# The order of the mixer's input projections: four output gate tiles placed between tiles with convolutions, and the triangular systems appended one tile sooner

## The chip, the cores and the metric

The kernel runs on one core of one Trainium2 chip. The metric is device time in microseconds. The kernel before took 2859.01 us, the median of 3 runs (2853.66 to 2862.34).

## What is computed

One layer of a decoder for 1024 prompt tokens and 8 sequences of 4 sample tokens, 1056 token columns in all, width 1024:

```
x += 1/2 * gate1 * SwiGLU1(mod(RMSNorm(x)))
h  = mod(RMSNorm(x))
qkv, z, b, a, q_raw, ckv_raw, kr_raw = split(h @ w_in)     # the input projection
qkv = silu(causal_conv(qkv)); q, k = l2_norm(q), l2_norm(k)
M   = strict_lower(beta * k k^T * decay);  T = inv(I + M)  # the triangular systems
o   = gated_delta_rule(q, k, v, T, ...) normed, times silu(z)
mla = attention over latents (q_raw, ckv_raw, kr_raw) and the paged cache
x += gate2 * [o, mla] @ w_out
x += 1/2 * gate3 * SwiGLU2(mod(RMSNorm(x)))
```

The change lies in the mixer's input projection `h @ w_in` and in what hangs on it.

## The kernel before

The features of `h` lie on the partitions, the 1056 token columns in four blocks of 264. The stage `mixer_in` (L1241) works through `w_in` in tiles of 128 columns. `ORDER` (L44) names them: `k0`..`k3`, `q0`..`q3` and `v0`..`v3` are the tiles of keys, queries and values that go through a convolution; `m0`..`m5` are the queries of the latent attention, `c0` its latents, and `z0`..`z3` the output gates. `I0` and `F0` are no tiles: they append side work to a list.

`proj` (L659) makes one tile: 4 blocks of 24 matmuls (each product in three parts, L127 to L129, out `pp`), and after each block an evacuation on ACT: L876 (`raw`) for k, q and v, L691 for m and c, L1228 (`zt<-pp`, a SiLU) for z. A z tile has no further work than one DMA, issued from ACT's queue (L1229). The weights of the tile two ahead are loaded on SP's queue (L648, `wraw`), cast on ACT (L652, `whi`), and their low parts are made on POOL (L101, `wlo`).

After each block `proj` calls `hook` (L682), which takes every generator on the list `active` one step further. So the side work is written between the blocks of later tiles:

- A tile of k, q or v appends its chain: `taps` (L881: ACT L893, three DVE passes L895, ACT L897 and L898), then nine transposes on PE (`ptk<-raw`, L701). For k and q follow the token norm (ACT L911, DVE L912, small DVE operations L707 to L720, DVE L920 `tok`), a scaling on POOL (`cy<-tok,egc`), transposes back on PE (`pch<-tok`, `pch<-cy`, L935), their evacuation (ACT L936) and products on PE (`pk`, L947).
- `I0` appends `invert` (L1040), which starts when all four k chains are done: masking on POOL (`M<-M,bi`), 31 steps of two DVE operations (`inv<-M` L1064, `M<-M,inv` L1066), and stores (POOL `X<-M,low`).
- `F0` appends nine times `mla_q_finish` (L1130), called F tiles below, three steps each, which start when the six m tiles are done: a load (SP, `mq<-qr_d`, L1138), squares (ACT L1140), sums and a root on DVE (L1143 to L1148), a scaling on POOL (`mq<-mq,g_q`), rotations on DVE and POOL (L1088 to L1093, `rp`), and a store (`qc_d<-mq`, L1153).

A framework lays the instructions out on every engine's queue by a schedule that it works out at build time; each queue then runs in that order. POOL is the exception: in this stage it keeps the order in which the code is written. The next stage, the attention of `mixer_heads`, begins when the last tile is done; its first transposes are `pqk` and `pqa`.

In a few words, of `mixer_in` and of `hook`:

```python
elif t[0] == "z":
    self.proj_z(m, tp, ps)
elif t[0] == "I":
    self.active.append(self.once("k", 4, self.invert(ml, tp)))
elif t[0] == "F":
    self.active.append(self.once("m", 6, self.in_turn([self.mla_q_finish(t, tp, ml) for t in range(NTL)])))
...
for g in list(self.active):
    if next(g, done) is done:
        self.active.remove(g)
```

Of the kernel before, what the change touches and what calls it, by code (L numbers as in the profile page):

```python
# [40 lines left out]
            ("T1", "S1", "Y", False), ("T4", "A22", "Z", True), ("B22", "S4", "Y", True))  # L41


ORDER = "k0 k1 m0 m1 k2 k3 c0 m2 I0 m3 m4 m5 F0 q0 q1 q2 q3 v0 v1 v2 v3 z0 z1 z2 z3"  # L44

PSQ = 3
WENG = 1
# [37 lines left out]
class Kernel:  # L85
# [1145 lines left out]
    def mixer_start(self):  # L1231
# [4 lines left out]
        first = {"k": 512, "q": 0, "v": 1024, "c": 2832, "m": 2064, "z": 1536}  # L1236
        self.worder = [[(2048, 16), (2960, 32)]] + [[(first[t[0]] + int(t[1]) * P, P)] for t in ORDER.split() if t[0] in first]
        while len(self.wready) < WFIRST:
            self.wready.append(self.proj_weights(WENG and self.nc.vector))

    def mixer_in(self):  # L1241

        nc, tc = self.nc, self.tc
        order = ORDER.split()
        c = self.keep
# [318 lines left out]
    def mla_prompt_gen(self, tp, ps):  # L1564
# [79 lines left out]
        def pv(h, qc, k, off, hi, lo):  # L1644

            vhi, vlo = va[h % 2]
            if k == 0:
                pas[h, qc] = ps.tile([P, 512], F32, tag="V", name="pa")
            last = k == ORDER[qc][-1]
            self.mm3(pas[h, qc][:, off:], vhi[:, k], vlo[:, k], hi[:, off:], lo[:, off:], k == 0, last)  # L1650
# [29 lines left out]

        ORDER = ((0, 3, 2, 1), (0, 7, 6, 5, 1, 2, 3, 4))

        def products(h):

            T = qk[h % 2]
            for qc in range(2):
                for k in ORDER[qc]:
                    off = max(0, k - 4 * qc) * P
# [569 lines left out]
```

## Time and profile before

| what | us |
|---|---|
| median of 3 runs | 2859.01 |
| the profiled execution, its own time | 2863.72 |
| its span, first to last instruction | 2861.9 |
| PE busy in the span | 2673.6 (93%) |
| DVE busy | 1766.6 (62%) |
| POOL busy | 1083.2 (38%) |
| ACT busy | 1074.2 (38%) |
| m2's first block to the end of z3 | 969 to 1286 |

PE runs the matmuls, PEld loads their weights, DVE, ACT and POOL do the elementwise work, SP issues DMAs. Times of rows are microseconds from the span's start. In brackets at a row's end stands how long the engine had been idle before it, and what it waited for. PEclk is the clock granted to PE, as a share of the full one.

### The profile page before, as it was taken

Reading aid. Unit: us, or ns where it says so; the run is one execution under the profiler, and the core shown is the slowest. Engines: PE = TensorE matmul, PEld = TensorE weight load, DVE = VectorE, ACT = ScalarE, POOL = GpSimd, SP = SyncE. Lnnn points to the kernel's source line nnn. Section 1 sums busy time; section 2 is a strip of 40 time slices with the busy share of each in tenths; the row PEclk is TensorE's granted clock in tenths of the full one; section 3 lists DMA queues with packets and bytes.
Section 4 is the critical chain, followed back from the end, with each engine's and each line's share of the span. In section 5 each row is a group of like instructions: output and inputs, shape, how many; then the busy total and the mean of one; then the engine's idle time right before and its main releaser. Section 6 shows DMA issues by size and latency. Waiting matters only on the chain.

```text
span 2861.9 us, 53475 instructions
## 1 busy us (share of the span) xinstructions
PE 2673.6 (93%) x21536; PEld 2462.5 (86%) x21536; DVE 1766.6 (62%) x3490; ACT 1074.2 (38%) x2005; POOL 1083.2 (38%) x1032
## 2 busy tenths in 40 slices
PE   4999999989999897799999988998979999999999
PEld 3888989989999787787877866776979999999999
DVE  7644445465574688847767677777585555546555
ACT  5322223211144443324656664543443333322111
POOL 0222222233352555544434466452433333323331
PEclk7999999999999998898999998987979999999999
DMA  7554353243232473432212144222522222224322
GB/s 272 154 163 134 120 162 105 81 161 106 76 109 77 149 206 117 141 110 78 63 42 58 49 96 114 83 64 53 188 82 82 76 87 71 90 82 167 98 76 69
DMA packets 339490, 308.35 MB, mean 108 GB/s; under 512 B 93865, under 2 KB 282017, under 8 KB 336171
## 3 DMA queue, kind: packets, MB, share of 16 engines
q1 hardware_dynamic: 304837, 246.32, 28.4%
q10 hardware_dynamic: 28262, 37.64, 4.1%
q0 software_dynamic: 6144, 20.98, 2.3%
q8 instruction: 169, 2.77, 0.4%
q14 instruction: 78, 0.64, 0.1%
HBM read 229.29 MB, written 75.59 MB: 107 GB/s over the span
## 4 chain that ended last, share of the span: by engine, by line
PE 42%; DVE 8%; issue 5%; POOL 4%; DMA 2%; ACT 1%; SPq 0%; ACTq 0%; POOLq 0%; DVEq 0%
PE po L128 4%; PE po L129 4%; PE po L127 4%; PE pY L127 2%; PE pY L128 2%; PE pY L129 2%; PE kraw L127 2%; PE pX L127 2%; PE pX L128 2%; PE pX L129 1%; PE pZ L127 1%; PE pZ L129 1%; PE pZ L128 1%; PE kraw L129 1%; PE kraw L128 1%
## 5 line engine op out<-in xcount | busy, mean ns | idle before, releaser
L127 PE MATMUL po<-act,whi 128*128 128x264 f32 x1408 | 402.4, 286 | 6.4 <-DVE x L435 4.7
L129 PE MATMUL po<-act,wlo 128*128 128x264 f32 x1408 | 403.2, 286 | 0.0
L128 PE MATMUL po<-act,whi 128*128 128x264 f32 x1408 | 402.0, 286 | 0.0
L435 DVE SCALAR_TENSOR_TENSOR x<-po,modT,x 128x264 f32<-128x264 f32 (+1 forms) x416 | 195.2, 480 | 238.8 <-PE po L129 238.3
L127 PEld LDWEIGHTS po<-act,whi 128*128 128x128 f32 x1408 | 266.8, 189 | 7.1 <-DVE x L435 4.9
L129 PEld LDWEIGHTS po<-act,wlo 128*128 128x128 f32 x1408 | 266.1, 189 | 0.0
L128 PEld LDWEIGHTS po<-act,whi 128*128 128x128 f32 x1408 | 265.9, 189 | 0.0
L370 POOL TENSOR_TENSOR A<-wg,A 128x512 fp32r<-128x512 f32 x84 | 111.0, 1321 | 372.1 <-ACT A L369 372.1
L127 PE MATMUL pp<-hhi,whi 128*128 128x264 f32 (+1 forms) x768 | 223.9, 292 | 4.5 <-DVE nt L354 3.6
L128 PE MATMUL pp<-hlo,whi 128*128 128x264 f32 (+1 forms) x768 | 223.7, 291 | 0.0
L129 PE MATMUL pp<-hhi,wlo 128*128 128x264 f32 (+1 forms) x768 | 221.8, 289 | 0.0
L2001 DVE TENSOR_REDUCE kss<-ksq 128x8 f32<-128x512 f32 x256 | 173.1, 681 | 69.7 <-ACT ksq L2000 67.7
L127 PE MATMUL pX<-B,A 128*128 128x264 f32 x704 | 203.9, 290 | 10.6 <-ACT B L369 9.7
L111 POOL TENSOR_TENSOR wlo<-wraw,whi 128x1024 fp32r<-128x1024 f32 x39 | 97.7, 2510 | 305.2 <-ACT whi L108 305.2
L2000 ACT ACTIVATE ksq<-kraw 128x512 f32<-128x512 f32 x256 | 152.1, 598 | 162.1 <-PE kraw L129 122.2
L128 PE MATMUL pX<-B,A 128*128 128x264 f32 x704 | 202.9, 288 | 8.9 <-DVE B L370 8.9
L128 PE MATMUL pY<-T,S 128*128 128x264 f32 x704 | 200.7, 285 | 1.6 <-DVE T L370 1.5
L129 PE MATMUL pX<-B,A 128*128 128x264 f32 x704 | 201.6, 286 | 0.0
L127 PE MATMUL pY<-T,S 128*128 128x264 f32 x704 | 200.3, 285 | 0.0
L129 PE MATMUL pY<-T,S 128*128 128x264 f32 x704 | 200.2, 284 | 0.0
L1700 POOL TENSOR_TENSOR plo<-pf,phi 128x512 fp32r<-128x512 f32 (+1 forms) x96 | 97.1, 1017 | 187.4 <-ACT phi L1699 169.7
L108 ACT CAST whi<-wraw 128x1024 fp32r<-128x1024 f32 x60 | 61.8, 1048 | 253.6 <-PE po L128 234.1
(538 smaller groups left out, 8305.1 us busy)
## 6 DMA issues: line engine op xcount, KB each, us to landing
adaw<-ada_w SPq DMA_DIRECT2D x72, 512.0 KB
wraw<-ffn_wi SPq DMA_DIRECT2D x46, 512.0 KB
act_d<-cc SPq DMA_DIRECT2D x88, 264.0 KB
wraw<-ffn_wo SPq DMA_DIRECT2D x44, 512.0 KB
wg<-ffn_wi SPq DMA_DIRECT2D x42, 512.0 KB
araw<-act_d ACTq DMA_DIRECT2D x160, 132.0 KB
x_d<-x SPq DMA_DIRECT2D x12, 1056.0 KB
wraw<-w_in SPq DMA_DIRECT2D x23, 512.0 KB
```

Source lines behind the costliest of these rows:

```text
L108: nc.scalar.copy(hi, raw)
L111: eng.tensor_tensor(out=lo, in0=raw, in1=f(hi), op=ALU.subtract)
L127: nc.tensor.matmul(out, whi, ahi, start=first, stop=False, **kw)
L128: nc.tensor.matmul(out, whi, alo, start=False, stop=False, **kw)
L129: nc.tensor.matmul(out, wlo, ahi, start=False, stop=last, **kw)
L370: eng.tensor_tensor(out=lo, in0=src, in1=f(hi), op=ALU.subtract)
L435: nc.vector.scalar_tensor_tensor(out=x[:, d, :n], in0=ps[:, :n], scalar=self.modT[:, m, d, 0:1], in1=x[:, d, :n], op0=ALU.mult, op1=ALU.add)
L1700: nc.gpsimd.tensor_tensor(out=lo[:, off:], in0=pf[:, off:], in1=f(hi[:, off:]), op=ALU.subtract)
L2000: nc.scalar.activation(sq, kr, AF.Square)
L2001: nc.vector.tensor_reduce(out=ss[:, (j * 4 + m) * H:(j * 4 + m + 1) * H], in_=sq.rearrange("p (h d) -> p h d", h=H), axis=AX.X, op=ALU.add)
```

## The change

One line, a list of names, is written in another order; no instruction is added or removed.

```diff
-ORDER = "k0 k1 m0 m1 k2 k3 c0 m2 I0 m3 m4 m5 F0 q0 q1 q2 q3 v0 v1 v2 v3 z0 z1 z2 z3"
+ORDER = "k0 k1 m0 m1 k2 k3 c0 I0 m2 m3 q0 m4 m5 z0 F0 q1 z1 q2 v0 q3 z2 v1 v2 v3 z3"
```

`I0` goes ahead of m2, q0 between m3 and m4, z0 ahead of `F0`, and z1, v0 and z2 between the other q tiles. z3 stays last. The weights' order follows the tiles' order. What moves on the queues is seen at three places.

PE, at the third q chain (`ptk` its transposes, `pk` the products of the q chain before it, `pp` projection matmuls). Before:

```order
L701 MATMUL ptk<-ident,raw 128x128 x8
L701 MATMUL ptk<-ident,raw 32x128
L947 MATMUL pk<-qT,kT 64x64 x16
L127 MATMUL pp<-hhi_9233,whi 128x264
L128 MATMUL pp<-hlo_9234,whi 128x264
L129 MATMUL pp<-hhi_9233,wlo 128x264
```

And now:

```order
L701 MATMUL ptk<-ident,raw 128x128 x8
L701 MATMUL ptk<-ident,raw 32x128
L128 MATMUL pp<-hlo_9234,whi 128x264
L129 MATMUL pp<-hhi_9233,wlo 128x264
L127 MATMUL pp<-hhi_9233,whi 128x264
```

The `pk` products of the chain before no longer stand behind these transposes; in the changed order that chain is over, 123 projection matmuls earlier. The number of rows on PE's queue from the last transpose `ptk` of a q chain to its first `pch<-tok`, without `pk` rows, goes from 60, 51, 30 and 34 for the four chains to 42, 100, 41 and 58. Of the 42, nine are products with 512 columns (`pkn`, `pv`).

ACT, at the gate tiles (`zt<-pp`, L1228). Before, they end the stage's queue:

```order
L893 ACTIVATE cy<-raw,convw 128x1080
L897 ACTIVATE raw<-cy 128x1024
L1228 ACTIVATE zt<-pp 128x264
L897 ACTIVATE raw<-cy 128x1024
L1228 ACTIVATE zt<-pp 128x264 x3
L1229 DMA z_d<-zt 128x1056
L652 CAST whi<-wraw 128x1024 x2
```

And now, for z2:

```order
L936 COPY raw<-pch 128x512 x2
L1140 ACTIVATE mqs<-mq 128x768
L897 ACTIVATE raw<-cy 128x1024
L898 ACTIVATE raw<-cy 128x32
L893 ACTIVATE cy<-raw,convw 128x1080
L1228 ACTIVATE zt<-pp 128x264 x3
L897 ACTIVATE raw<-cy 128x1024
L1228 ACTIVATE zt<-pp 128x264
L652 CAST whi<-wraw 128x1024
```

Its evacuations now stand among the taps of q3 and v0 and the squares of an F tile.

POOL, from the low part of one tile's weights (`wlo`) to that of the next, in the stretch with F tiles (`mq`, `rp`) and q chains (`cy`). Before:

```order
L101 TENSOR_TENSOR wlo<-wraw,whi 128x256 x4
L906 MEMSET tss 128x2
L101 TENSOR_TENSOR mq<-mq,g_q 128x192 x4
L1089 TENSOR_TENSOR rp<-mq,k_rope 128x128
L1091 TENSOR_TENSOR rp<-mq,k_rope 128x128
L101 TENSOR_TENSOR cy<-tok,egc 128x4x64 x4
L888 COPY ncv<-raw 128x3
L889 COPY ncv<-raw 128x24
L101 TENSOR_TENSOR wlo<-wraw,whi 128x256 x4
```

And now:

```order
L101 TENSOR_TENSOR wlo<-wraw,whi 128x256 x4
L101 TENSOR_TENSOR mq<-mq,g_q 128x192 x4
L1089 TENSOR_TENSOR rp<-mq,k_rope 128x128
L1091 TENSOR_TENSOR rp<-mq,k_rope 128x128
L101 TENSOR_TENSOR mq<-mq,g_q 128x192 x4
L888 COPY ncv<-raw 128x3
L889 COPY ncv<-raw 128x24
L101 TENSOR_TENSOR wlo<-wraw,whi 128x256 x4
```

Between two tiles' weights stand F tiles alone, where a scaling `cy` of a q chain stood in every such piece before. The masking `M<-M,bi` of the triangular systems has also moved on POOL, from behind the copies of c0's chain to ahead of them.

## The prediction

> **What bounds the kernel now.** I read the clock first, then the windows of the stage, cut where the last matmul of a tile ends.
>
> ```profile
> core 0: 2861.9 us, clock 0.955
> 969.00:1059.00 90.00, 79.22 (x756) 74.56 (x755) 62.38 (x178) 39.18 (x82) 51.46 (x84) 0.92 0.80 223
> 1059.00:1100.00 41.00, 39.35 (x317) 38.13 (x315) 39.77 (x102) 16.93 (x36) 22.17 (x33) 1.00 0.42 136
> 1100.00:1213.00 113.00, 81.35 (x741) 75.81 (x742) 92.71 (x233) 39.94 (x88) 64.75 (x77) 0.82 0.40 134
> 1213.00:1243.00 30.00, 26.99 (x214) 26.64 (x213) 25.55 (x41) 10.28 (x21) 19.85 (x23) 0.94 0.40 135
> 1243.00:1262.00 19.00, 15.68 (x118) 15.34 (x118) 5.88 (x15) 3.92 (x8) 11.88 (x22) 0.91 0.39 120
> 1262.00:1286.00 24.00, 24.00 (x204) 23.82 (x203) 1.49 (x3) 3.52 (x9) 2.14 (x3) 1.00 0.24 82
> sum 317.00, PE 266.59 PEld 254.30 DVE 227.77 ACT 113.78 POOL 172.26; mean PE 44.43 PEld 42.38 DVE 37.96 ACT 18.96 POOL 28.71
> ```
>
> The columns after the length are PE, PEld, DVE, ACT and POOL busy, then the granted clock. The rows are m2 to m5; q0 to q2; q3 to v2; v3 and z0; z1; z2 and z3. Four tiles take 113 us in the third row and two take 24 in the last, where PE is never idle and DVE has 1.49 us of work. So the stage has two faults side by side: a stretch in which the side work holds PE up, and an end with nothing beside PE. PE is idle for 317.00 - 266.59 = 50.4 us, 31.7 of them in the third row. The waits of PE in 969 to 1286 name the causes.
>
> ```profile
> PE pch L935 <- DVE tok L920: 23.1, 4, 6.2
> PE ptk L701 <- ACT raw L898: 7.8, 2, 4.5
> PE pch L935 <- POOL cy L101: 6.7, 5, 2.4
> PE ptk L701 <- ACT raw L897: 6.0, 4, 3.0
> ```
>
> Nearly half is one wait, once for each q chain: the transposes back (`pch`) for the normed tokens (`tok`). The timelines of SP, ACT, DVE and PE show how it comes about in q1's chain.
>
> ```profile
> 1118.22 1.20 PE L701 MATMUL ptk<-ident,raw 128*128 128x128 f32 x9 [0.49 <-ACT raw L897]
> 1119.95 0.32 SPq L1153 DMA_DIRECT2D qc_d<-mq  x1
> 1120.38 0.37 SPq L1138 DMA_DIRECT2D mq<-qr_d  x1
> 1126.07 0.85 ACT L1140 ACTIVATE mqs<-mq 128x768 f32<-128x768 f32 x1 [3.78 <-DMA mq<-qr_d]
> 1126.82 0.25 ACT L911 ACTIVATE tsq<-ptk 32x128 f32<-32x128 f32 x1
> 1126.94 1.01 DVE L1143 TENSOR_REDUCE hs<-mqs 128x8 f32<-128x512 f32 x2 [4.42 <-ACT mqs L1140]
> 1132.63 2.21 DVE L920 TENSOR_TENSOR tok<-tok,trs 128x1024 f32<-128x1024 f32 x2
> 1134.39 1.94 PE L935 MATMUL pch<-ident,tok 128*128 128x128 f32 x8 [6.21 <-DVE tok L920]
> ```
>
> The F tile's load stands behind the F tile's last store on SP, ACT waits for it, and the q chain's last squares (1126.82) stand behind that on ACT; DVE then interleaves both roots. From the transposes' end at 1119.4 to `pch` at 1134.4 are 15.0 us, and the 51 matmuls in between cover only part. After such a gap PE also runs at a lower clock.
>
> **The change, part by part.** No work is added or removed, so the stage keeps PE's 266.59 us less what the clock takes. Each window's PE time by its shortfall of clock: 79.22 x 0.08 = 6.3, 81.35 x 0.18 = 14.6, 26.99 x 0.06 = 1.6, 15.68 x 0.09 = 1.4, together 24. At full clock and without a wait the stage would take about 243 us, DVE's work is 228. Hence there is room, up to a bound, and the gain is what of the 50 + 24 us goes.
>
> *The wait for `tok`, 23.1 us.* A block of 24 matmuls takes 2.90 us at full clock, by the evacuations in z2 and z3:
>
> ```profile
> 1273.69 0.39 ACT L1228 ACTIVATE zt<-pp 128x264 f32<-128x264 f32 x1 [2.51 <-PE pp L129]
> 1285.29 0.39 ACT L1228 ACTIVATE zt<-pp 128x264 f32<-128x264 f32 x1 [2.51 <-PE pp L129]
> 1105.02 1.97 PE L935 MATMUL pch<-ident,tok 128*128 128x128 f32 x8 [5.19 <-DVE tok L920]
> 1162.21 1.94 PE L935 MATMUL pch<-ident,tok 128*128 128x128 f32 x8 [6.02 <-DVE tok L920]
> 1191.56 1.94 PE L935 MATMUL pch<-ident,tok 128*128 128x128 f32 x8 [5.69 <-DVE tok L920]
> ```
>
> (11.60 us for four blocks, 0.121 us a matmul.) The cover goes from 60, 51, 30, 34 rows to 42, 100, 41, 58. If every chain keeps its latency, the four waits of 5.19, 6.21, 6.02 and 5.69 change by +2.2 (less 0.8 for nine wider products), -5.9, -1.3 and -2.9 us, to 6.6, 0.3, 4.7 and 2.8: 14.4 are left, a gain of 8.7. If the latencies shrink too, because q0's chain now runs ahead of the F tiles, and a second q chain no longer shares DVE and ACT with the first, all 23.1 can go. I take 14, somewhat under the middle, since F tiles and triangular steps stay beside q1 to q3.
>
> *The wait for `cy`, 6.7 us.* Only at q0 do 26 matmuls now stand between `pch<-tok` and `pch<-cy`; its wait goes, the others remain: 1.4.
>
> ```profile
> 1108.35 2.14 PE L935 MATMUL pch<-ident,cy 128*128 128x128 f32 x8 [1.36 <-POOL cy L101]
> 973.80 0.28 PE L701 MATMUL ptk<-ident,raw 128*32 128x128 f32 x1 [4.52 <-ACT raw L898]
> 991.07 1.62 PE L701 MATMUL ptk<-ident,raw 128*128 128x128 f32 x8 [1.99 <-ACT raw L897]
> 1224.23 1.97 PE L701 MATMUL ptk<-ident,raw 128*128 128x128 f32 x8 [3.01 <-ACT raw L897]
> 1247.17 0.29 PE L701 MATMUL ptk<-ident,raw 128*32 128x128 f32 x1 [3.33 <-ACT raw L898]
> ```
>
> *The waits for `raw`, 13.8 us.* The 4.52 and 1.99 belong to k chains, ahead of what moves, and stay. The other 7.3 are transposes that stood too close behind their taps; in the changed order at least 64 matmuls, 7.7 us, follow each v tile before its transposes. Bounds 0 and 7.3; I take 6, nearer the upper end.
>
> *The clock.* Over 1100 to 1262 it costs 14.6 + 1.6 + 1.4 = 17.6 us beside 23.1 + 6.3 us of these waits, 0.6 us lost per us waited. (14 + 1.4 + 6) x 0.6 gives 12.8, at most 17.6, at least 5 for the 8.7 alone; I take 12. The row beside it: 0.82 of full clock with four gaps above 5 us, against 1.00 in 1059 to 1100. [...]
>
> *The end of the stage.* z3 alone now covers v3's chain. Here are v3's last evacuation, DVE's last operation on its transposes, and what followed z3:
>
> ```profile
> 1230.28 0.35 ACT L876 COPY raw<-pp 128x232 f32<-128x232 f32 x1 [2.64 <-PE pp L129]
> 1252.97 0.28 DVE L1035 COPY cy<-ptk 32x128 f32<-32x128 f32 x1 [2.30 <-PE ptk L701]
> 1285.71 0.33 ACTq L1229 DMA_DIRECT2D z_d<-zt  x1
> 1292.09 1.91 PE L1768 MATMUL pqa<-qsTt,wukTt 64*128 64x32 f32 x8 [4.48 <-DVE wukTt L1764]
> ```
>
> The chain took 22.7 us, among two other v chains and an F tile; z3 and its store cover about 14. Alone it should need less; the bounds are 0 and 9, and I charge 2. The 4.48 us gap behind z3 stays.
>
> *The moved gate tiles and queues.* Their sixteen evacuations (16 x 0.39 = 6.2 us) go onto ACT where it is a third busy (39.94 of 113), and four stores of 0.33 us stand on ACT's queue ahead of the next squares. Their weights pass SP and POOL in the crowded stretch; POOL's part is dearer there:
>
> ```profile
> 1004.47 2.83 POOL L101 TENSOR_TENSOR wlo<-wraw,whi 128x256 fp32r<-128x256 f32 x4
> 1141.63 6.00 POOL L101 TENSOR_TENSOR wlo<-wraw,whi 128x256 fp32r<-128x256 f32 x4
> ```
>
> That is up to 3.2 us more for each of three, on a POOL that is 57% busy there and works two tiles ahead; what queues behind is an F tile's `mq` or a `cy`. Bounds 0 and 9.5; I charge 3, for the `cy` waits. This row, DVE's taps against POOL, speaks against the change. [...]
>
> *The triangular systems.* `M<-M,bi` stands earlier on POOL, where it may wait for the load of `M`, and copies and weights queue behind it; the weights have two tiles of slack. DVE's steps end earlier, but nothing waited for them: cost and gain 0, up to 3 either way.
>
> The sum: 14 + 1.4 + 6 + 12 - 2 - 3 = 28 us. The stage goes from 317 to 289, with PE at 243/289 and DVE at 228/289 = 79%, less than the 97% of 1059 to 1100. The profiled execution took 2863.72 us (span 2861.9 and 1.8 around it) and would take 2835.7. It lies 4.7 above the median of the runs, so I forecast 2859.0 - 28 = 2831. This case's own bounds: 23.1 + 1.4 + 7.3 of waits and 17.6 of clock less 2 of charges, 47, so 2812; and 8.7 + 5 of gains less 5 of charges, about 9, so 2850.
>
> **The rivals.** *Each chain keeps its price.* A q chain holds PE up because of its own sequence over four engines, and a gate tile beside it hides nothing: the waits keep their 23 us, and the gaps only move to other places. For it: DVE is 82% busy over 1100 to 1213 (92.71 of 113), and the waits come from queues in fixed order, not from a lack of PE work. Against it: 100 matmuls, 12 us, now cover q1's 15. Time: within 9 us of 2859.
>
> *The F tiles set the pace; slower.* They must pass one after another, and POOL's rows show their steps:
>
> ```profile
> 1086.23 2.97 POOL L101 TENSOR_TENSOR mq<-mq,g_q 128x192 f32<-128x192 f32 x4 [13.48 <-ACT raw L897]
> 1094.65 3.15 POOL L101 TENSOR_TENSOR mq<-mq,g_q 128x192 f32<-128x192 f32 x4
> 1214.33 4.29 POOL L101 TENSOR_TENSOR mq<-mq,g_q 128x192 f32<-128x192 f32 x4 [1.02 <-issue]
> 1241.99 2.25 POOL L101 TENSOR_TENSOR mq<-mq,g_q 128x192 f32<-128x192 f32 x4 [9.14 <-issue]
> ```
>
> From the first to the ninth are 155.8 us, 19.5 a tile. `F0` now follows z0 instead of m5, so the F tiles start about 32 us later (two more tiles at 41/3 = 13.7 us and 5 us of q0's chain), near 1091, and end in v1, with 3.25 tiles or 41 us at 12.7 to go. The stage ends at 1091 + 9p + 41: with p = 19.5 at 1307, 21 us later than 1286, and the kernel takes 2880. It decides from p = 17.1. Against it: the first two lie 8.4 us apart, before a q chain was in the way; the 20 us came with tiles of 28 us, so the pace looks like an effect. My forecast needs p = 14.
>
> *The change doesn't do what it says.* The queues show that it does; no chance of its own.
>
> **How the numbers follow.** A measurement of this kernel can tell about 0.3%, 8.6 us, from no change. I give the forecast's case 0.78 (2812 to 2850, most likely 2831), the case that chains keep their price 0.12, and the F tiles' pace 0.10. The first is all faster; a part of the second, 0.01, is as well, and of the third 0.01 lies within. So faster 0.79, same 0.12, slower 0.09. The range reaches from 2812 into the second case, to 2858, and leaves out about 0.04 below and 0.15 above.
>
> **What would show it.** Right: the window of q1 to v1 with PE at 90% and a clock near 0.95; `pch<-tok` waits of 10 us or less in sum; `mq` rows on POOL 13 to 15 us apart; v3's chain ending within a few us of z3. Wrong: `mq` rows still 19 us apart (the F tiles' pace), waits for `tok` still above 20 us in sum (the chains keep their price), or a gap of over 5 us more at the stage's end.

## The result, and the profile after

| | us, median | runs | against before, 95% interval |
|---|---|---|---|
| before | 2859.49 (2853.66 to 2862.34) | 4 | |
| changed | 2838.32 (2834.46 to 2840.12) | 4 | 0.9927 (0.9907 to 0.9946) |

The changed kernel is 21 us faster (15 to 27); 28 had been forecast, for a time of 2831 us. Two more comparisons, each with the kernel before on the same chip, gave 0.9939 (0.9919 to 0.9958) and 0.9958 (0.9941 to 0.9975), so 17 and 12 us. The profiled execution took 2839.8 us, of a span of 2838.0.

The windows of the changed stage, cut again at tiles' ends (PE, PEld, DVE, ACT, POOL busy, then the granted clock): m2 to m5 with q0; z0 and q1; z1, q2 and v0; q3, z2 and v1; v2 and v3; z3.

```profile
core 0: 2838.0 us, clock 0.957
968.00:1072.00 104.00, 94.53 (x858) 88.81 (x858) 75.63 (x220) 44.90 (x95) 60.46 (x91) 0.92 0.72 206
1072.00:1115.00 43.00, 33.56 (x295) 32.62 (x294) 39.74 (x76) 13.58 (x30) 14.91 (x22) 0.88 0.47 152
1115.00:1156.00 41.00, 39.94 (x378) 39.25 (x378) 34.14 (x84) 16.79 (x37) 25.55 (x36) 1.00 0.44 147
1156.00:1217.00 61.00, 45.82 (x395) 44.31 (x393) 47.94 (x130) 21.86 (x44) 38.09 (x57) 0.89 0.43 143
1217.00:1252.00 35.00, 32.08 (x293) 31.48 (x294) 23.95 (x45) 12.56 (x31) 19.62 (x29) 0.90 0.29 97
1252.00:1266.00 14.00, 13.80 (x116) 13.45 (x115) 7.97 (x15) 4.30 (x9) 0.99 (x4) 1.00 0.18 55
sum 298.00, PE 259.73 PEld 249.93 DVE 229.36 ACT 114.00 POOL 159.63; mean PE 43.29 PEld 41.65 DVE 38.23 ACT 19.00 POOL 26.61
```

The stage went from 317 to 298 us. PE's idle time fell from 50.4 to 38.3 (298 - 259.73), its busy time, in which the clock's loss lies, from 266.59 to 259.73. What a gate tile can do shows in the third row: z1, q2 and v0 pass in 41 us with PE at 97% and a full clock, and q1's chain, which lies there, does not hold PE up. What is left shows in the fourth, with q2's chain in it: 15 us idle at 0.89.

PE's largest waits in the changed stage, and that for `cy`:

```profile
PE pch L935 <- DVE tok L920: 16.4, 3, 8.9
PE ptk L701 <- ACT raw L897: 5.9, 2, 5.2
PE ptk L701 <- ACT raw L898: 4.6, 1, 4.6
PE ptk L701 <- DVE dml L948: 4.3, 1, 4.3
PE pch L935 <- POOL cy L101: 1.9, 2, 1.0
```

The waits for `tok` are down by 6.7 us, those for `cy` by 4.8, those for `raw` from 13.8 to 10.5; the wait of 4.3 for `dml` is new.

Then the long pieces of the program: from c0's last product to z3's last evacuation (the stage), and on to the first product of the scan (the attention's stretch). Before:

```profile
969.30:1285.30 316.00, 265.60 (x2329) 253.57 (x2330) 227.77 (x569) 113.40 (x243) 171.96 (x238) 0.90 0.50 155
1285.30:1722.10 436.80, 419.36 (x2532) 340.81 (x2532) 311.67 (x583) 268.73 (x528) 205.29 (x236) 0.97 0.26 67
1722.10:1987.90 265.80, 239.93 (x2652) 185.07 (x2653) 197.25 (x409) 116.61 (x239) 137.05 (x155) 0.88 0.29 78
```

And changed:

```profile
967.60:1265.40 297.80, 259.37 (x2326) 249.80 (x2326) 229.20 (x565) 113.61 (x242) 159.90 (x236) 0.92 0.51 157
1265.40:1703.40 438.00, 420.94 (x2535) 341.98 (x2533) 313.16 (x587) 269.58 (x528) 208.09 (x238) 0.97 0.28 72
1703.40:1962.50 259.10, 235.65 (x2653) 181.58 (x2654) 201.44 (x409) 117.09 (x239) 137.39 (x155) 0.89 0.30 80
```

The stage gave 18.2 us, the attention's stretch took 1.2 back. The third rows, the scan, differ by 6.7 us, which can't be put down to the change: in the profiles below the scan takes 255 to 274 us at a clock of 0.85 to 0.93, and 256.2 to 263.9 us in three profiles of the changed kernel alone. So the sum of stage and stretch, 752.8 us before, is compared from here on.

### The profile page after: what moved, and what is told of

Read it like the earlier page. It is cut to its first block, busy times and chain, and to the rows that moved or that the text cites. A ratio compares the mean times of both kernels' runs of the same rounds, so it can differ in the third digit from the quotient of the medians.

```text
span 2838.0 us, 53470 instructions
## 1 busy us (share of the span) xinstructions
PE 2663.8 (94%) x21536; PEld 2455.5 (87%) x21536; DVE 1772.1 (62%) x3490; ACT 1076.1 (38%) x2005; POOL 1075.4 (38%) x1032
## 4 chain that ended last, share of the span: by engine, by line
PE 71%; DVE 13%; issue 5%; POOL 5%; DMA 4%; ACT 2%; SPq 0%; ACTq 0%; DVEq 0%; POOLq 0%
PE po L127 7%; PE po L129 7%; PE po L128 7%; PE pY L127 4%; PE pY L128 4%; PE pY L129 4%; PE pX L127 3%; PE pX L128 3%; PE pX L129 3%; PE pZ L127 3%; PE pZ L128 3%; PE pZ L129 3%; POOL gt L101 2%; PE pp L127 1%; PE pp L128 1%
## 5 line engine op out<-in xcount | busy, mean ns | idle before, releaser
L127 PE MATMUL pX<-B,A 128*128 128x264 f32 x704 | 204.1, 290 | 10.6 <-ACT B L369 9.7
```

Of the source, the lines that this page charges most:

```text
L127: nc.tensor.matmul(out, whi, ahi, start=first, stop=False, **kw)
```

## The experiments

All in one table; the first reduction is the attention's first softmax maximum on DVE, counted from z3's last evacuation.

| kernel | stage | to the first reduction | stretch | sum against 752.8 | whole kernel against before (95%) |
|---|---|---|---|---|---|
| before | 316.0 | 14.0 | 436.8 | | |
| changed | 297.8 | 17.3 | 438.0 | -17.0 | 0.9927 (0.9907 to 0.9946) |
| after_again | 297.5 | 17.3 | 438.1 | -17.2 | 0.9939 (0.9919 to 0.9958) |
| after_third | 298.3 | 18.2 | 444.0 | -10.5 | 0.9958 (0.9941 to 0.9975) |
| z_only | 302.2 | 19.6 | 441.6 | -9.0 | 0.9986 (0.9969 to 1.0003) |
| i_only | 312.6 | 7.9 | 425.8 | -14.4 | 0.9968 (0.9949 to 0.9986) |
| z_end | 315.3 | 8.4 | 427.4 | -10.1 | 0.9973 (0.9958 to 0.9989) |
| before_ring | 314.5 | 7.9 | 423.2 | -15.1 | 0.9968 (0.9956 to 0.9980) |
| after_ring | 303.4 | 21.0 | 438.3 | -11.1 | 0.9936 (0.9919 to 0.9952) |
| burst_dve | 298.4 | 17.8 | 435.7 | -18.7 | 0.9957 (0.9941 to 0.9973) |
| f_first | 311.1 | 17.4 | 437.4 | -4.3 | 0.9995 (0.9981 to 1.0009) |
| f_later | 303.8 | 17.0 | 439.2 | -9.8 | 0.9968 (0.9951 to 0.9986) |
| end_two | 298.6 | 8.1 | 423.6 | -30.6 | 0.9919 (0.9893 to 0.9946) |
| end_two_2 | 301.0 | 7.9 | 424.4 | -27.4 | 0.9918 (0.9896 to 0.9940) |

A profile is one execution, the ratio comes from 4 to 12 runs. One per cent of the ratio is 28.6 us; seen so, the two columns agree to a few us in most rows, and where they don't the profiles mostly show more (before_ring 15 by its profile, 6 to 13 by its runs). The one profile of before lies 4.7 us above the median of its runs, and those of before_ring, after_ring, burst_dve, after_third and end_two are the fastest executions of theirs. The stages and stretches are compared by place, the kernels by their ratios.

**The parts one by one.** The theory was that gate tiles' matmuls laid over the q chains' waits bring the time; the rivals were the earlier q0, and the earlier triangular systems.

```diff
-ORDER = "... c0 m2 I0 m3 m4 m5 F0 q0 q1 q2 q3 v0 v1 v2 v3 z0 z1 z2 z3"
+ORDER = "... c0 m2 I0 m3 m4 m5 F0 q0 z0 q1 z1 q2 z2 q3 v0 v1 v2 v3 z3"    (z_only)
+ORDER = "... c0 I0 m2 m3 m4 m5 F0 q0 q1 q2 q3 v0 v1 v2 v3 z0 z1 z2 z3"    (i_only)
+ORDER = "... c0 I0 m2 m3 q0 m4 m5 F0 q1 q2 v0 q3 v1 v2 v3 z0 z1 z2 z3"    (z_end)
```

> Only the gate tiles move (z0, z1, z2 behind q0, q1, q2; I0, q0, v0 and F0 stand as before). Cover theory (the gain is matmuls of gate tiles laid over the q chains' waits and over the stretch in which DVE is the busier engine): most of the 21 us, so 12 to 20 us less than before, about 2843; PE idle in the stage falls from 50 us to about 40, the waits for tok to about 15 us. Rival, the earlier q0 brings it (its chain runs ahead of the F tiles): under 6 us, about 2855, since q0 stands behind F0 here as before. Rival, the earlier triangular systems bring it: within 3 us of before.

> Only I0 is ahead of m2, all else as before. Cover theory, and the term of the prediction: no change, within 3 us of 2859. Rival, the triangular systems' DVE steps, ended one tile sooner, leave DVE free for the q chains: 6 us or more less than before, and the waits for tok below 18 us.

> The changed order with z0, z1, z2 back at the end; I0, q0 and v0 stay moved. Cover theory: the gain is mostly gone, 0 to 8 us less than before, about 2855, with DVE nearly idle in the last 40 us of the stage as before. Rival, the earlier q0 (and v0 among the q tiles) brings it: 12 us or more less than before, about 2843.

> The changed kernel once more, for a second profile. Theory: the stage from m2's first block to z3's end is again 298 us (295 to 301), and the stall of 11 us of one triangular step on DVE, beside the low parts of three tiles' weights on POOL, is there again, since the queues' order makes it; the stretch of the scan (259 us from its first to its last product, against 266 before) varies from run to run and may be 259 or 266. Rival, the stall is an accident of one execution: the operation takes under 4 us, and the stage is 7 to 10 us shorter.

In the stage the theory holds: the gate tiles alone take 13.8 of the 18.2 us, everything but them takes 0.7, by one profile each; three profiles of the changed stage lie within 0.8 us. In z_only PE's idle time fell to 39.8 us, as expected, the waits for `tok` to 18.0, not to 15. With q0 and v0 moved and no gate tile between, the waits for `tok` even grew from 23.1 to 27.8. In the whole kernel it fell: z_only gained 4 us, not 12 to 20, and I0 alone gained 9, where nothing was expected. Both differences lie behind the stage. The attention's stretch is 5 us longer in z_only, and 11 and 9 shorter in i_only and z_end. The rival on the triangular systems does not explain it either: in i_only the waits for `tok` are 18.9 us, but those for `cy` 10.4 instead of 6.7, and the stage itself gained 3.4. after_again gave the stage and the stall (11.11 us) as expected, so neither is an accident of one execution.

**What stands behind the stage.** These are DVE's and POOL's rows of the kernel before, at the attention's start:

```profile
1288.61 0.48 DVE L1775 MEMSET zero<- 128x512 f32 x1 [10.14 <-DMA z_d<-zt]
1289.14 1.04 POOL L635 DMA_INDIRECT krh<-cache_krope,idx  x1 [24.65 <-ACT vhi L1627]
```

`zero` is cleared where z3's gate tile lay (byte 92288 of a partition, the gate tile from 92192), and must wait for the gate tile's store; DVE's casts and copies stand behind it, and on one of them, `wukTt`, PE's gap of 4.48 us. The gate tile's buffer is one of a ring of ten, and which one it gets depends on how many buffers were taken before it, so any edit of the order can change it. The next two kernels shift the ring and leave the order alone:

```diff
+for _ in range(2):      (before_ring; 4 in after_ring)
+    self.nc.gpsimd.memset(self.r(tp, [P, NT], "skip")[:, :2], 0.0)
```

> The order of before; two buffers of the stage's ring of ten are taken and cleared (2 columns each) ahead of m2, so that z3's gate tile lies in another buffer, which the next stage takes over late. Handover theory (with I0 alone moved, the gain lay behind the stage: the first DVE operations of the attention no longer waited for the store of the last gate tile, whose buffer they take over): the stage keeps 316 us, from z3's last evacuation to the first softmax reduction it is 8 to 9 us instead of 14.0, and up to 5 us more come in the attention, whose gathers start earlier; 6 to 11 us less than before in all, about 2850. Rival, the earlier triangular systems themselves brought it: within 3 us of before, and the 14.0 us stay.

> The changed kernel with four buffers of the ring taken and cleared ahead of m2, so that z3's and v3's last tiles lie in buffers that the attention's first operations do not take over. Handover theory: from z3's last evacuation to the first softmax reduction 9 to 13 us instead of 17.3, the attention's gathers start earlier, 4 to 9 us less than the changed kernel, about 2832. Rival, v3's chain with its stores on SP's queue sets the start of the attention: the 17 us stay, within 3 us of the changed kernel (2840).

The same two operations in before_ring (its lines are numbered two higher):

```profile
1257.41 0.48 DVE L1777 MEMSET zero<- 128x512 f32 x1
1261.08 0.95 POOL L635 DMA_INDIRECT krh<-cache_krope,idx  x1 [0.30 <-issue]
```

They run 24 and 20 us before z3's last evacuation (1281.6). The start fell from 14.0 to 7.9 us, the stretch by 13.6, the whole kernel by 9 (6 to 13), in the order of before. More is lost there than PE's gap of 4.48 us. These are the first 50 us behind z3's last evacuation, before and then in before_ring:

```profile
1285.30:1299.30 14.00, 9.52 (x56) 8.63 (x57) 7.82 (x22) 3.12 (x6) 7.77 (x8) 0.73 0.67 211
1299.30:1310.30 11.00, 10.49 (x61) 9.03 (x60) 4.08 (x15) 1.04 (x2) 6.54 (x6) 0.50 0.50 165
1310.30:1335.30 25.00, 25.00 (x121) 20.52 (x121) 20.57 (x35) 16.22 (x33) 5.09 (x9) 0.89 0.14 34
```

```profile
1281.60:1295.60 14.00, 13.47 (x110) 12.12 (x110) 11.19 (x33) 5.68 (x10) 5.68 (x6) 0.88 0.72 237
1295.60:1306.60 11.00, 10.97 (x55) 8.76 (x54) 6.09 (x11) 4.48 (x8) 6.66 (x9) 1.00 0.11 25
1306.60:1331.60 25.00, 24.64 (x142) 20.80 (x141) 23.75 (x48) 18.00 (x36) 3.49 (x4) 1.00 0.12 32
```

PE is idle for 5.0 us before and 0.9 in before_ring. By the shortfall of its clock, reckoned as in the prediction, it loses 10.6 and 1.6 us. Together these are 13.1 of the 13.6 us, most of them clock. In all nine profiles with a start of 14 us or more the clock of the middle row, 14 to 25 us behind z3, is 0.50 or 0.51, in the five with a start of about 8 us 0.80 to 1.00.

So the handover theory is shown for the order of before. In i_only the clearing of `zero` has moved as well, to 6.7 us ahead of z3's last evacuation (1279.7):

```profile
1273.03 0.48 DVE L1775 MEMSET zero<- 128x512 f32 x1
```

Its gain behind the stage is thus the handover's, which before_ring brings without moving the triangular systems.

In the changed order the theory failed: after_ring is where the changed kernel is, its scan begins at 1704.1 against 1703.4 (its c0 ended 5 us sooner, so its stage reads longer). A handover is there too, since DVE's first operation of the attention waits for the store of v3's last tile, and PE behind it. after_ring took it away, and PE then waited longer for `mtok`, a load, and began the products `pqk` at the same time (1273.96; the changed kernel, after a wait of 0.94 us, at 1273.64). There the rival holds. DVE's, SP's and PE's rows of the changed kernel at the end of v3's chain, and PE's of after_ring:

```profile
L1035 DVE COPY cy<-ptk x4: 269/269/279, 1201.2 to 1264.4; 32x128 f32<-32x128 f32 x4
1264.95 0.65 SPq L956 DMA_DIRECT2D smp_d<-cy  x1
1268.74 0.39 SPq L1595 DMA_DIRECT2D mtok<-qc_d  x1
1268.47 0.69 DVE L1748 TENSOR_TENSOR wukf<-wukh,wukl 128x512 f32<-128x512 f32 x1 [1.95 <-DMA vb_d<-cy]
1270.01 0.84 PE L1755 MATMUL pqg<-ident,qg 32*96 32x32 f32 x8 [4.21 <-DVE qg L1751]
```

```profile
1273.96 1.91 PE L1607 MATMUL pqk<-ident,mtok 128*96 128x128 f32 x8 [3.99 <-DMA mtok<-qc_d]
```

v3's chain ends with z3, its stores and four more pass SP first, and the loads of the attention (`mtok`) come behind them.

**Two gate tiles at the end.** If that is so, v3's chain needs more cover, not another buffer.

```diff
-ORDER = "... q3 z2 v1 v2 v3 z3"
+ORDER = "... q3 v1 v2 v3 z2 z3"
```

> The changed order with z2 taken from between q3 and v1 to the end, next to z3, so that v3's chain ends under two gate tiles (25 us) instead of one. Theory (in the changed kernel v3's late chain and its stores set the start of the attention: 17.3 us from z3's last evacuation to the first softmax reduction, and gathers that start only at 1266): that piece falls to 7 to 10 us and the stretch from z3's end to the first product of the scan from 438 to 423 to 428 us; the stage loses z2's cover for q3's chain and takes 298 to 306; in all 4 to 14 us less than the changed kernel, about 2831. Rival, what z2 covers at q3 is worth as much as what it brings at the end: within 3 us of 2840.

The same opening in end_two, on DVE and PE:

```profile
1256.46 0.67 DVE L1750 TENSOR_TENSOR qg<-qs,g_kn 32x512 f32<-32x512 f32 x1
1269.60 1.08 PE L1768 MATMUL pqa<-qsTt,wukTt 64*128 64x32 f32 x8 [0.53 <-DVE wukTt L1764]
```

The opening operations lie under z2 and z3, PE's gap is 0.53 us, the stretch 423.6. The table shows the same: every order that ends with a single gate tile needs 17 us or more to the first reduction, every one that ends with two or four about 8, but for before with its handover. And z2 is hardly missed in its old place: the stage takes 298.6, and 301.0 in the second run of this order. Once more, on one chip with the changed kernel:

> The order with z2 and z3 last once more, on the same chip as the changed kernel, to tell the two apart. Theory: the stretch from z3's last evacuation to the first product of the scan is again 14 us shorter (424 against 438), the stage the same 298; 8 to 14 us less than the changed kernel by the medians. Rival: within 3 us of it, the 14 us being given back in the scan or after it.

> The changed kernel on the same chip: 0.9927 to 0.9939 of before, as in its other runs; the stage 298 us, the stretch to the first product of the scan 438.

There the medians were 2842.83 and 2856.55, 13.7 us apart, the stretches 424.4 and 444.0 us, and the two intervals of the ratio just fail to meet (to 0.9940, from 0.9941). The changed kernel missed its own expectation, 0.9958 and 444.0 us instead of 0.9939 at most and 438, so part of the distance is that it was slower this time. This order beats both kernels; by the changed kernel's other ratios, 0.9927 and 0.9939, it would be by 2 to 6 us only, less than their intervals can tell.

**DVE beside POOL's weights.** In the changed kernel the low parts of three tiles adjoin on POOL's queue, and one triangular step on DVE looks like this:

```profile
1079.30 11.13 DVE L1066 TENSOR_TENSOR M<-M,inv 128x480 f32<-128x480 f32 x1
1081.60 8.32 POOL L101 TENSOR_TENSOR wlo<-wraw,whi 128x256 fp32r<-128x256 f32 x12
```

burst_dve makes these three on DVE.

```diff
-self.wready.append(self.proj_weights())
+self.wready.append(self.proj_weights(self.nc.vector if self.worder[0][0][0] in (128, 256, 1664) else None))
```

> The changed kernel with the low parts of q1's, z1's and q2's weights made on DVE (three operations of 128x1024) instead of in twelve pieces on POOL. Stall theory (POOL's twelve pieces back to back hold one DVE operation up for 11 us, and the transposes of q0's chain wait for that): the longest operation of L1066 is under 4 us, the wait of 4.3 us at 1095 is gone, z0 takes 20 to 23 us instead of 31, the stage 288 to 292 us instead of 298; about 2832. Rival, the 11 us are made good by what waits later in the F tiles and chains: z0 is shorter, but the stage stays within 3 us of 298, about 2839.

The same operation there, and in f_first, where two tiles' low parts adjoin:

```profile
1080.30 0.66 DVE L1066 TENSOR_TENSOR M<-M,inv 128x480 f32<-128x480 f32 x1
```

```profile
1078.51 8.39 DVE L1066 TENSOR_TENSOR M<-M,inv 128x480 f32<-128x480 f32 x1
1080.81 5.57 POOL L101 TENSOR_TENSOR wlo<-wraw,whi 128x256 fp32r<-128x256 f32 x8
```

The stall goes, and the stage does not move (298.4). The wait for `dml` is gone, but the wait for q0's `tok`, behind the same low parts on DVE, is 9.9 us instead of 5.0, and z0 is not shorter: its last evacuation is at 1104.86, against 1104.15 in the changed kernel. The whole kernel is no better than the changed one. The stall theory fell in this form: the 11 us are real, and taking them away by more work on DVE brings no time. Whether another place for the weights would bring the 4.3 us of `dml` was not tried.

**The place of F0.**

```diff
-ORDER = "... m5 z0 F0 q1 z1 q2 ..."
+ORDER = "... m5 F0 z0 q1 z1 q2 ..."    (f_first)
+ORDER = "... m5 z0 q1 F0 z1 q2 ..."    (f_later)
```

> The changed order with F0 ahead of z0 instead of behind it. Theory of the F tiles as a co-bound (they start at 1114 in the changed kernel, and eight of them at 15 us end in v3): they start about 11 to 14 us earlier, the q chains wait about as long, and the stage is 3 to 8 us shorter, about 2834. Rival, the pace of PE with its waits sets the end and the F tiles have slack: the stage stays within 3 us of 298, about 2839; or F tiles fall among q0's chain and its waits grow: 3 to 6 us longer.

> The changed order with F0 behind q1 instead of ahead of it: the F tiles start one tile later. With F0 one tile earlier the stage had grown by 13 us. Theory (an F tile beside a q chain lengthens that chain on DVE, ACT and SP, so the later they start the better): q2's wait for tok falls from 9 us to 5 or less, the stage is 3 to 8 us shorter, about 2834. Rival, the F tiles are then the last to end: nine at 15 us from about 1127 end near 1262, the loads of their results hold up the attention's first transposes, and the kernel is 3 to 10 us slower than the changed one, about 2846.

Both are worse, by 13 and 6 us in the stage. PE's waits for `tok` there, f_first and then f_later:

```profile
PE pch L935 <- DVE tok L920: 23.0, 4, 10.5
```

```profile
PE pch L935 <- DVE tok L920: 23.3, 3, 13.3
```

Neither theory covers both sides. With the F tiles earlier the waits grow from 16.4 to 23.0 us, but that later is better is refuted by f_later, whose longest wait for `tok`, 13.3 us, falls on q2's chain, like the 8.95 of the changed kernel. My guess is that it matters which step of an F tile meets which step of a chain; no run shows it.

## Why the prediction was right, and where it was not

The mechanism is in the main the one it named, gate tiles between the chains, and the time lies in its range. The sum was too large: 28 against 17 in stage and stretch. That the whole came as near as 21 is in part luck: of the 23.9 us between the two profiled executions 6.7 lie in the scan, and the other two comparisons gave 17 and 12.

*The wait for `tok`* (14 taken, 8.7 to 23.1): 6.7 came, less than the lower end. The four waits, forecast by the cover alone as 6.6, 0.3, 4.7 and 2.8, were 5.0, 0, 8.95 and 2.4. That three of the four came near is in part luck, for the cover is the step that failed. Here are the second q chain (q1's) before, between its transposes and its `pch`, and then in the changed kernel:

```profile
1119.36 1.15 PE L947 MATMUL pk<-qT,kT 64*64 64x64 f32 x32
1121.62 1.15 PE L947 MATMUL pk<-qT,kT 64*64 64x64 f32 x32
```

```profile
1125.83 1.15 PE L701 MATMUL ptk<-ident,raw 128*128 128x128 f32 x9
1138.93 1.03 PE L935 MATMUL pch<-ident,tok 128*128 128x128 f32 x8
```

Before, 64 `pk` rows of the chain ahead stood in that place for each of the last three chains; now none do, and the count of rows had left `pk` out. Measured as time, from a chain's last transpose to the start of PE's wait, the cover went from 7.2, 8.8, 6.2 and 6.7 us to 6.1, 12.0, 5.4 and 7.0: 1.6 more in sum, where 8.7 were forecast. Less 0.121 us for each row that was counted (51, 30 and 34), `pk` had given 2.6 us to each of the three. The other step, "if the latencies shrink too", for which the 14 held 5.3, came true in sum: from the last transpose to `pch` the chains took 12.4, 15.0, 12.2 and 12.4 us before and 11.1, 12.0, 14.4 and 9.4 after, 5.1 less. Only q2's grew. Its rows show why, on PE, POOL and DVE:

```profile
1167.79 2.18 PE L701 MATMUL ptk<-ident,raw 128*128 128x128 f32 x9 [5.17 <-ACT raw L897]
1167.55 3.03 POOL L101 TENSOR_TENSOR wlo<-wraw,whi 128x256 fp32r<-128x256 f32 x4
1170.55 2.81 POOL L101 TENSOR_TENSOR X<-M,low 128x256 f32<-128x256 f32 x4
1170.65 0.65 DVE L711 SCALAR_TENSOR_TENSOR hs<-hs 128x16 f32<-128x16 f32 x1
1173.64 0.17 DVE L710 SCALAR_TENSOR_TENSOR hs<-hs 128x16 f32<-128x16 f32 x1
1175.00 0.68 DVE L912 TENSOR_REDUCE tss<-tsq 128x8 f32<-128x512 f32 x1
1184.33 1.94 PE L935 MATMUL pch<-ident,tok 128*128 128x128 f32 x8 [8.95 <-DVE tok L920]
```

An F tile's root of small operations stands ahead of the chain's first sum on DVE, and while POOL makes low parts and masks (1167.6 to 1173.4) each of them takes 0.65 us or more instead of 0.17; seven of them make 3.4 us. From the transposes' end (1169.97) to `pch` are 14.4 us, 2.2 more than before for this chain.

*`cy`*: 4.8 came, 1.4 was taken. *`raw`*: 3.3 came, not 6; the step looked at v tiles, and the new wait is q2's (5.17 above). *The wait for `dml`*, 4.3 us, is new and was not forecast.

*The clock* (12 taken): PE's busy time fell by 6.9; by the windows' shortfall (7.6 + 4.0 + 5.0 + 3.2 = 19.8, before 24) it is 4.2. The rate of 0.6 us per us waited was applied to 21 us of waits, and only 12.1 of PE's idle time went; 12.1 x 0.6 is 7.3, near the 6.9, but by the shortfall, from which the rate was taken, it is 0.35. So the base failed, and whether the rate held stays open. Nor did the long waits get fewer: of PE's waits above 4 us in the stage five stand before (5.19, 6.21, 6.02, 5.69, 4.52) and five after (5.02, 8.95, 5.17, 4.55, 4.32). In the 3 us behind each of them the granted clock was 0.50, 0.50, 0.50, 0.50 and 0.60 before, and 0.50, 0.50, 0.50, 0.61 and 0.56 after.

*The end of the stage* (2 charged, "the 4.48 us gap behind z3 stays"): 3.3 us were lost to the first reduction, within the bounds. But the gap before was not a fixed price. It was a buffer's, and 13.6 us of the stretch, most of them clock, went with it in before_ring. In the changed kernel v3's late chain takes its place, at about the same price, and end_two shows the 14 us that this leaves on the table. Taking that gap as given was the costliest omission.

*The weights on POOL* (3 charged for `cy`): the price fell on DVE, 11.13 us in one operation and the wait for `dml`, and burst_dve could not turn it into time. *The triangular systems* (0, up to 3): 3.4 us of the stage when moved alone.

*The rivals.* "Each chain keeps its price": not so, 18 us of the stage went, though q2's chain by itself behaves in that way. "The F tiles set the pace": POOL's first and ninth scaling are 122.2 us apart, 15.3 a tile, below the 17.1 from which it would decide.

```profile
1114.16 2.38 POOL L101 TENSOR_TENSOR mq<-mq,g_q 128x192 f32<-128x192 f32 x4 [24.25 <-DVE mq L1148]
1236.39 2.27 POOL L101 TENSOR_TENSOR mq<-mq,g_q 128x192 f32<-128x192 f32 x4 [10.31 <-DVE mq L1148]
```

They started at 1114, not near 1091, since z0 took 31 us. Of the signs named, v3's chain does end within 1 us of z3, and the clock from q1 to v1 is 0.94:

```profile
1103.30:1216.70 113.40, 97.46 (x868) 95.26 (x866) 91.08 (x247) 42.60 (x88) 64.19 (x93) 0.94 0.41 139
```

But PE is busy there for 86%, not 90 (97.46 of 113.4), the pace missed 15 by a little, and the waits for `tok` were 16.4 us instead of 10.

## What to carry to other kernels

Work without a chain behind it is worth most where a chain keeps the main engine waiting, but keep enough of it for the end: here the last chain had to finish, with its stores, under cover, or the next stage paid. When cover is counted, count also what leaves the place. When an order changes, look also at which buffers the last tiles get and who takes them over, since a gain or a loss of 10 us may come from that alone. A part tried alone should be read stage by stage, because the causes of its gain can lie outside the stage that was changed.

## What the runs showed of the hardware

One DVE operation with two inputs, `M<-M,inv` of 128x480, lasted as long as a whole run of POOL operations beside it, not as long as a single one: it took 11.13 us beside a run of four `cy` and twelve `wlo`, 8.39 beside four and eight (f_first), and 0.66 without the run (burst_dve). Both times it ended 0.5 us after the run's last operation, and with the run of twelve it took 11.11 in after_again and in after_third and 11.13 in end_two_2. Yet in the changed kernel's rows of q2's chain, between POOL's pieces of 0.7 us, the operations of 128x16 got through, one per piece (0.65 us each, and 0.17 once POOL's pieces had ended at 1173.4). Why the two differ no run here shows.
